# Transfers of ScalarE's results issued by ScalarE itself, in a two-layer attention, delta-rule and Fourier backbone

## The chip, the cores and the metric

The kernel runs on one core of a Trainium2 chip. The metric is the device time of one execution in microseconds; before the change the median of three runs is 2653.78 us. The core's engines work side by side, each through its own queue of instructions in a fixed order: TensorE (PE in the profile) multiplies matrices, VectorE (DVE), ScalarE (ACT) and GpSimd (POOL) do elementwise work, and SyncE (SP) issues transfers between the main memory and the on-chip memory. Semaphores tie the queues together: an instruction that waits for a result of another engine holds up everything behind it on its own.

## The reference: what is computed

512 latent tokens and 256 context tokens, 1024 channels each, pass through two layers. In each layer, one wide projection of the normalised tokens feeds three mixers side by side; their results are gated, merged and added, and a squared-ReLU MLP follows. Cut to what matters here:

```python
h_l = _rmsnorm(x, norm1) * (1 + sc1) + sh1
(na_k, na_v, dn_k, dn_v, dn_a, dn_b, na_q, dn_q, dn_z, fn_u, gate) = _split(h_l @ w_in, ...)
# A: 8x16 neighbourhood attention plus all context keys, one softmax, 8 heads of 64
o_na = _neighbourhood_attention(q * scale, k, v, kc, vc, rpb)
# B: gated delta rule in both directions, 4 heads of 128, in chunks
g = -exp(a_log) * softplus(dn_a + dt_bias);  beta = sigmoid(dn_b)
o_dn = _gated_head_norm(ol_f + ol_b, dn_z, dn_norm)
# C: real part of a 2-D Fourier transform over positions and channels, 4 groups of 128
o_fn = _fourier(fn_u)
# merge
g_na, g_dn, g_fn = split(sigmoid(gate))
y = (g_na * (o_na @ w_na_o) + g_dn * (o_dn @ w_dn_o) + g_fn * (o_fn @ w_fn)) @ w_out
x = x + gt1 * y
x = x + gt2 * (square(relu(rmsnorm(x) @ w_mlp1)) @ w_mlp2)
```

Context tokens go through the same mixers and, in the first layer only, through the merge and the MLP as well; in the second layer they only give keys, values and delta-rule states.

## The kernel before

**Layout and precision.** Activations lie with channels on the partitions and tokens along the free axis: 768 columns, 512 latent and 256 context ones (TT; TL is 512, TC is 256). Every large product is done in three passes with operands split in a rounded main part and a remainder: weights (`wr` as loaded, `whi` and `wlo` as split) and activations (`hh`, `hl`). `wload` (L233 and on) loads a weight block of 128x512 on SP, ScalarE casts it to `whi` (L243), and VectorE or GpSimd makes `wlo` (L246). So each projection on TensorE (`ps_in`, `ps_inc`, L255) waits for a load, a cast on ScalarE and a subtraction.

**Stages.** A layer has a mixing stage (projection and the three mixers, mixed with each other), a merge and an MLP. In mixing, the transform runs first, with the first delta-rule head (`fourier` and `dn_in`). Then four streams run together: the delta rule's steps (`stream_dn`), its preparation (`stream_prep`, `dn_prep`: products of keys, decay factors, triangular solve), the attention (`stream_na`, `na_attn`) and the projections (`stream_in`: queries, keys and values of attention, delta-rule inputs, and the first 16 of the 24 blocks of gates).

**What sets the order.** `by_clock` takes from the four streams in turn, by a clock that the streams advance themselves, and gives delta-rule code a higher priority. A scheduler of the framework then sets the order of each engine's queue: it goes by the code's order and priorities, the waits between instructions and its own cost estimates. Which engine issues a transfer is thus an input to it. Transfers share eight completion semaphores, used in turn by all of them.

**The transfers that the change touches.** All are issued by SP, in one queue with the weight loads:

- L462: the decay sums (`gdr` from `gct`, 48x128), a copy made by ScalarE, once per layer. `dn_prep` reads them back for each head at L542 and L543 (`Df`, `Db`, spread over 128 partitions). GpSimd adds masks (L549 to L551) and ScalarE makes 18 exponentials of 128x128 out of them (L556 to L558).
- L750: the gates (`gpre` from `sgp`), 16 blocks in each layer; a sigmoid in several steps ends on ScalarE (L128). They are read again in the merge.
- L793: the queries. `raw` holds two heads on 64 partitions each. For each half, ScalarE makes the main part `qd` (L790), VectorE the remainder `ql` (L791), and two transfers copy each to the other 64 partitions. The scores (L841, L842) read both.
- L880: the attention's result (`ona` from `o_na`), one store for each of four pairs of heads in a layer; its last part is a copy on ScalarE.
- L961: the transform's result (`ofn`, and `ofnn` for the last 4 rows, from `o_fn`), five tiles for the latent part and, in the first layer, five for the context part; copies on ScalarE.

`gct`, `o_fn` and some others share one small ring of buffers (tag `t2`): a buffer is free again when its store has landed.

In attention, `na_pair` takes two heads at a time: their scores (`ps_s`), a softmax on VectorE and ScalarE (`Pm`, L809 to L820), transposes on TensorE (L825, against `ident`), a copy, and the product with the values (L831).

Of the kernel before, what the change touches and what calls it, by code (L numbers as in the profile page):

```python
# [9 lines left out]
F32 = mybir.dt.float32  # L10
# [7 lines left out]
P = 128  # L18
# [20 lines left out]
FNC, FNW, FAW = (0, TL // 2 + 2), (TL + TC) // 2 + 4, 264  # L39
# [7 lines left out]
def kernel(ctx: ExitStack, tc: tile.TileContext, A: dict, out: bass.AP):  # L47
# [327 lines left out]
    def layer(l):  # L375
        full = l == 0
        segs = ALL if full else LAT
        W = TT if full else TL
# [36 lines left out]
        def gates():  # L415
            ab_f = tp.tile([P, TT], F32, tag="t3", name="ab_f")
            for v, (s0, s1) in enumerate(ALL):
                ps, k0 = (ps_aux("ps_ab"), 0) if l else (begun["ab"][v], KD // 2)
                proj_ab(ps, hh, hl, s0, s1, k0, KD)
                act.copy(ab_f[0:32, s0:s1], ps[0:32, 0:s1 - s0])  # L420
            pab = ps_aux("ps_ab2")
            for j in range(6):
                pe.matmul(pab[:, 16 * j:16 * j + 16], lhsT=ab_f[0:32, j * P:(j + 1) * P], rhs=selab, start=True, stop=True)
            abv = pab[:, 0:96].rearrange("p (j c) -> p j c", c=16)
            for nm in ("z", "g", "beta", "gc", "tot", "egc", "tail", "etot", "t0", "nbe", "btail", "ngc"):
                G[nm] = sm.tile([P, 6, 8], F32, tag="g_" + nm, name="g_" + nm)
            alog = rows[l][:, 0:1, :].to_broadcast([P, 6, 8])
            dtb = rows[l][:, 1:2, :].to_broadcast([P, 6, 8])
            ea = sm.tile([P, 8], F32, tag="g_ea", name="g_ea")
            act.activation(out=ea, in_=rows[l][:, 0, :], func=AF.Exp)  # L430
            dve.tensor_tensor(G["z"], abv[:, :, 0:8], dtb, op=ALU.add)
            dve.tensor_scalar(G["t0"], G["z"], -1.0, None, op0=ALU.mult)
            dve.tensor_tensor(G["btail"], G["z"], G["t0"], op=ALU.max)
            act.activation(out=G["t0"], in_=G["btail"], func=AF.Exp, scale=-1.0)
            act.activation(out=G["t0"], in_=G["t0"], func=AF.Ln, bias=1.0)
            dve.scalar_tensor_tensor(G["t0"], in0=G["z"], scalar=0.0, in1=G["t0"], op0=ALU.max, op1=ALU.add)
            dve.scalar_tensor_tensor(G["g"], in0=G["t0"], scalar=-1.0, in1=ea.unsqueeze(1).to_broadcast([P, 6, 8]),
                                     op0=ALU.mult, op1=ALU.mult)
            sigmoid_into(G["beta"], abv[:, :, 8:16])
            pg = ps_aux("ps_g")  # L440
            gflat = G["g"].rearrange("p j c -> p (j c)")
            for i, m in enumerate((m_ui, m_li, ones)):
                pe.matmul(pg[:, 48 * i:48 * i + 48], lhsT=m, rhs=gflat, start=True, stop=True)
            pgv = pg[:, 0:144].rearrange("p (i j c) -> p i j c", i=3, c=8)
            act.copy(G["gc"][:, :, 0:4], pgv[:, 0, :, 0:4])
            act.copy(G["gc"][:, :, 4:8], pgv[:, 1, :, 4:8])
            act.copy(G["tot"], pgv[:, 2])
            dve.tensor_scalar(G["ngc"], G["gc"], -1.0, None, op0=ALU.mult)
            act.activation(out=G["egc"], in_=G["gc"], func=AF.Exp)
            act.activation(out=G["etot"], in_=G["tot"], func=AF.Exp)  # L450
            dve.tensor_tensor(G["t0"], G["tot"], G["gc"], op=ALU.subtract)
            act.activation(out=G["tail"], in_=G["t0"], func=AF.Exp)
            dve.tensor_tensor(G["btail"], G["beta"], G["tail"], op=ALU.mult)
            dve.scalar_tensor_tensor(G["nbe"][:, :, 0:4], in0=G["egc"][:, :, 0:4], scalar=-1.0, in1=G["beta"][:, :, 0:4],
                                     op0=ALU.mult, op1=ALU.mult)
            dve.tensor_scalar(G["nbe"][:, :, 4:8], G["egc"][:, :, 4:8], -1.0, None, op0=ALU.mult)

            pgt = ps_aux("ps_gt")
            pe.transpose(pgt[0:48, 0:P], G["gc"].rearrange("p j c -> p (j c)"), ident)
            gct = tp.tile([P, 512], F32, tag="t2", name="gct")  # L460
            act.copy(gct[0:48, 0:P], pgt[0:48, 0:P])
            sp.dma_start(out=gdr, in_=gct[0:48, 0:P])  # L462


        odn = drp.tile([NDH, P, TT], F32, tag="odn", bufs=1, name="odn")
# [277 lines left out]
        def pre_gates():  # L743
            for k in range(NPRE):
                ps = inproj(T_GATE + k, segs)
                sg = tp.tile([P, TT], F32, tag="t3", name="sgp")
                gl = U("gl", tag="cy", w=774)
                evac(gl, ps)
                sigmoid_into(sg[:, :W], gl[:, :W])
                sp.dma_start(out=gpre[k, :, :W], in_=sg[:, :W])  # L750
                yield IN_T[l]


# [2 lines left out]
        def na_in(c, st):  # L756

            halves = (slice(0, 64), slice(64, P))
            ps = inproj(T_NAK + c, ALL)
            raw = tp.tile([P, TT], F32, tag="t3", name="kraw")  # L760
            act.copy(raw[:, 0:TL].rearrange("p (t r c) -> p t r c", t=4, c=16),
                     ps[0].rearrange("p (r t c) -> p t r c", r=8, c=16))
            act.copy(raw[:, TL:TT], ps[1][:, 0:TC])
            ks = [U("ks", F32R, tag="n") for _ in range(2)]
            for t, r, r2 in zip(ks, halves, halves[::-1]):
                act.copy(t[r], raw[r])
                dve.tensor_tensor(t[r2], raw[r], t[r].bitcast(F32), op=ALU.subtract)
            yield IN_T[l]
            ps = inproj(T_NAV + c, ALL)
            vN = tp.tile([P, TT], F32, tag="t3", name="vN")  # L770
            act.copy(vN[:, 0:TL].rearrange("p (t r c) -> p t r c", t=4, c=16),
                     ps[0].rearrange("p (r t c) -> p t r c", r=8, c=16))
            act.copy(vN[:, TL:TT], ps[1][:, 0:TC])
            vt = tok_major(vN, OFF, "naV", tag="n")
            yield IN_T[l]
            ps = inproj(T_NAQ + c, segs)
            raw = tp.tile([P, TT], F32, tag="t3", name="qraw")
            pq = ps[0].rearrange("p (r c) -> p r c", c=64)
            act.activation(out=raw[:, P:TL].rearrange("p (t r c) -> p t r c", t=3, c=16),
                           in_=pq[:, :, 8:56].rearrange("p r (t c) -> p t r c", c=16), func=AF.Copy, scale=0.125)  # L780
            act.activation(out=raw[:, 0:P].rearrange("p (r a b) -> p r a b", r=8, b=8),
                           in_=ps[0].rearrange("p (r a b) -> p r a b", r=8, b=8)[:, :, 0:8:7, :], func=AF.Copy,
                           scale=0.125)
            if full:
                act.activation(out=raw[:, TL:TT], in_=ps[1][:, 0:TC], func=AF.Copy, scale=0.125)

            qd = [U("qd", F32R, tag="n") for _ in range(2)]
            ql = [U("ql", F32R, tag="n") for _ in range(2)]
            for t, lo, r, r2 in zip(qd, ql, halves, halves[::-1]):
                act.copy(t[r, :W], raw[r, :W])  # L790
                dve.tensor_tensor(lo[r, :W], raw[r, :W], t[r, :W].bitcast(F32), op=ALU.subtract)  # L791
                for x in (t, lo):
                    sp.dma_start(out=x[r2, :W].bitcast(F32), in_=x[r, :W].bitcast(F32))  # L793
            st.update(ks=ks, vt=vt, qd=qd, ql=ql)
            yield IN_T[l]

# [39 lines left out]
        def na_attn(c, st):  # L836
# [34 lines left out]
            if full:  # L871
                for qi in range(2):
                    def scores(hh):
# [3 lines left out]

                    yield from na_pair(scores, 0, (None, None), [vt[:, 4], vt[:, 5]],
                                       o[:, TL + qi * P:TL + (qi + 1) * P], lambda t: t)
            sp.dma_start(out=ona[c, :, :W], in_=o[:, :W])  # L880

# [4 lines left out]
        def fourier():  # L888
# [35 lines left out]
            for i, (s0, n, tab) in enumerate(sets):  # L924
# [26 lines left out]
                for x, c0, c1 in ((0, 0, P), (0, P, 2 * P), (1, 0, P), (1, P, 2 * P), (0, 256, 260)):  # L951
                    m = c1 - c0
                    ps = ps_aux("ps_fb", "fb")
                    for r, (w, f) in enumerate(ab[x]):
                        for y, (a, b) in enumerate(((0, 0), (0, 1), (1, 0))):
                            pe.matmul(ps[0:m, :nh], lhsT=w[a][:, c0:c1], rhs=f[b][:, :nh], start=(r == 0 and y == 0),
                                      stop=(r == len(ab[x]) - 1 and y == 2))
                    o = tp.tile([P, 512], F32, tag="t2", name="o_fn")
                    act.copy(o[0:m, :nh], ps[0:m, :nh])
                    dst = ofnn if m == 4 else ofn[2 * x + c0 // P]  # L960
                    sp.dma_start(out=dst[:, FNC[i]:FNC[i] + nh], in_=o[0:m, :nh])  # L961
                    yield 2


# [403 lines left out]
```

## Time and profile before

| what | value |
| --- | --- |
| median of three runs | 2653.78 us (2650.65 to 2654.24) |
| the profiled execution | 2646.47 us, of which its span 2644.6 us |
| TensorE busy | 2460.2 us (93%), 14608 matmuls |
| VectorE, ScalarE, GpSimd busy | 1533.8, 1211.9, 650.3 us |
| mean granted TensorE clock | 0.975 of full speed |
| TensorE busy, 100 to 745 us (mixing, layer 0) | 591.58 of 645 us |
| TensorE busy, 1550 to 2117 us (mixing, layer 1) | 504.68 of 567 us |

The busy time of an engine doesn't count what it issues as transfers. Such issues appear as "SPq" in a timeline, that is, as work of SP's sequencer, with the time that the issuing took; when the data have landed is a separate figure. A wait row names the waiting instruction by engine, tile and line, then what came last of all that it waited for, the total in microseconds, how often, and the longest. In a timeline, the bracket at a row's end is the idle time of the engine before it, and what ended it.

### The profile page before, as it was taken

What the parts mean: (1) busy time and instruction counts of PE and PEld (TensorE: products, weight loads), DVE (VectorE), ACT (ScalarE), POOL (GpSimd) and SP (SyncE); (2) the same over time, 40 slices, a digit from 0 to 9 for tenths busy, and PEclk for the clock granted to TensorE, in tenths of its full rate; (3) what the DMA queues carried; (4) which work ended last, traced back from release to release, by engine and by line L of the source; (5) the groups of instructions that cost most, each with busy time, mean ns of one, the idle gap of its engine ahead of it and who ended that gap; (6) DMA issues with size and microseconds to landing.
All of it is one profiled execution on the core that took longest, in us unless ns stands there. A gap on an engine that the chain in (4) does not pass through costs nothing. (4 is left out here: it accounts for less than half of the span.)

```text
span 2644.6 us, 39355 instructions
## 1 busy us (share of the span) xinstructions
PE 2460.2 (93%) x14608; PEld 2039.8 (77%) x14608; DVE 1533.8 (58%) x3035; ACT 1211.9 (46%) x2573; POOL 650.3 (25%) x536
## 2 busy tenths in 40 slices
PE   6988999899998999999999988898889999999998
PEld 3876877777887878888888867676777777788886
DVE  4627676757557967564434473857677457433334
ACT  4545657565654233131313255555566763423333
POOL 3222223231122122111111133322333232222222
PEclk9999999999999999999999999999999999999999
DMA  6233132323154743334333313332222345233332
GB/s 222 67 83 87 60 77 75 86 78 86 55 182 149 225 145 109 126 111 127 119 127 112 124 62 95 86 77 71 75 84 80 99 143 191 80 96 96 96 96 87
DMA packets 188807, 280.90 MB, mean 106 GB/s; under 512 B 57876, under 2 KB 78104, under 8 KB 188488
## 3 DMA queue, kind: packets, MB, share of 16 engines
q1 hardware_dynamic: 188616, 278.40, 34.7%
q8 instruction: 114, 1.87, 0.3%
q14 instruction: 77, 0.63, 0.1%
HBM read 242.86 MB, written 26.03 MB: 102 GB/s over the span
## 5 line engine op out<-in xcount | busy, mean ns | idle before, releaser
L246 POOL TENSOR_TENSOR wlo<-wr,whi 128x512 fp32r<-128x512 f32 x352 | 497.5, 1416 | 1670.5 <-ACT whi L243 1550.0
L243 ACT CAST whi<-wr 128x512 fp32r<-128x512 f32 x544 | 335.5, 619 | 783.6 <-PE ps_m L255 490.8
L255 PE MATMUL ps_in<-hh,whi 128*128 128x512 f32 x960 | 378.2, 405 | 26.9 <-ACT whi L243 21.3
L255 PE MATMUL ps_in<-hh,wlo 128*128 128x512 f32 x960 | 374.3, 400 | 2.6 <-POOL wlo L246 2.5
L255 PE MATMUL ps_in<-hl,whi 128*128 128x512 f32 x960 | 374.7, 401 | 0.0
L255 PE MATMUL ps_m<-mh,whi 128*128 128x512 f32 (+1 forms) x768 | 232.3, 357 | 4.7 <-ACT mh L319 4.7
L255 PE MATMUL ps_m<-ml,whi 128*128 128x512 f32 (+1 forms) x768 | 233.5, 358 | 2.8 <-POOL ml L323 2.3
L255 PE MATMUL ps_m<-ah,whi 128*128 128x512 f32 (+1 forms) x776 | 233.5, 354 | 0.0
L255 PE MATMUL ps_m<-al,whi 128*128 128x512 f32 (+1 forms) x776 | 233.1, 354 | 0.0
L255 PE MATMUL ps_m<-ah,wlo 128*128 128x512 f32 (+1 forms) x776 | 233.0, 354 | 0.0
L255 PE MATMUL ps_m<-mh,wlo 128*128 128x512 f32 (+1 forms) x768 | 232.6, 356 | 0.0
L255 PEld LDWEIGHTS ps_in<-hh,whi 128*128 128x128 f32 x960 | 180.9, 193 | 58.8 <-ACT whi L243 22.3
L246 DVE TENSOR_TENSOR wlo<-wr,whi 128x512 fp32r<-128x512 f32 x192 | 135.7, 707 | 138.7 <-ACT whi L243 138.6
L255 PEld LDWEIGHTS ps_in<-hh,wlo 128*128 128x128 f32 x960 | 180.3, 192 | 37.4 <-POOL wlo L246 5.6
L255 PEld LDWEIGHTS ps_in<-hl,whi 128*128 128x128 f32 x960 | 180.9, 193 | 29.8 <-issue 1.7
L1198 DVE SCALAR_TENSOR_TENSOR x<-ps_m,mod,x 128x512 f32<-128x512 f32 (+1 forms) x97 | 60.8, 654 | 215.4 <-PE ps_m L255 215.4
L202 DVE SCALAR_TENSOR_TENSOR jada<-wada,csb 128x1024 f32<-128x1024 f32 x128 | 179.7, 1404 | 0.8 <-DMA wada<-in_wat_dram 0.4
L255 PEld LDWEIGHTS ps_m<-ml,whi 128*128 128x128 f32 x768 | 127.8, 190 | 27.7 <-POOL ml L323 5.1
L255 PE MATMUL ps_inc<-hh,wlo 128*128 128x256 f32 x512 | 149.2, 291 | 0.0
L255 PE MATMUL ps_inc<-hl,whi 128*128 128x256 f32 x512 | 149.1, 291 | 0.0
L255 PEld LDWEIGHTS ps_m<-mh,whi 128*128 128x128 f32 x768 | 127.8, 190 | 27.6 <-ACT mh L319 6.4
L255 PE MATMUL ps_inc<-hh,whi 128*128 128x256 f32 x512 | 148.7, 290 | 0.1
(338 smaller groups left out, 4962.8 us busy)
## 6 DMA issues: line engine op xcount, KB each, us to landing
wr<-in_w_dram SPq DMA_DIRECT2D x256, 256.0 KB, 2.6
wr<-in_wi_dram SPq DMA_DIRECT2D x224, 256.0 KB, 2.7
wada<-in_wat_dram SPq DMA_DIRECT2D x80, 512.0 KB, 3.9
wr<-in_wb_dram SPq DMA_DIRECT2D x48, 256.0 KB, 3.1
wada<-in_wa_dram SPq DMA_DIRECT2D x32, 256.0 KB, 5.4
wr<-in_wo_dram SPq DMA_DIRECT2D x32, 256.0 KB, 2.8
gpre<-sgp SPq DMA_DIRECT2D x16, 384.0 KB, 2.3
sgg<-gpre SPq DMA_DIRECT2D x16, 384.0 KB, 4.1
```

Of the source, the lines that this page charges most:

```text
L202: pin(dve.scalar_tensor_tensor(junk, in0=ws[n], scalar=1.0, in1=cur["csb"][:, v * D:v * D + D], op0=ALU.mult, op1=ALU.mult, accum_out=MOD[ ...
L243: act.copy(hi, raw)
L246: eng.tensor_tensor(lo, raw, hi.bitcast(F32), op=ALU.subtract)
L255: pe.matmul(ps[:, s0 - off:s1 - off], lhsT=a, rhs=b[k][:, s0:s1], start=(k == 0 and i == 0), stop=(k == kn - 1 and i == 2))
L1198: dve.scalar_tensor_tensor(x2[k][:, s0:s1], in0=ps[:, s0:s1], scalar=mod(l, 5, k, v), in1=x2[k][:, s0:s1], op0=ALU.mult, op1=ALU.add)
```

## The change

Five places take their transfer from SP to ScalarE. At L793, only the main part of the queries moves, which ScalarE makes; the remainder, made by VectorE, stays on SP.

```diff
             act.copy(gct[0:48, 0:P], pgt[0:48, 0:P])
-            sp.dma_start(out=gdr, in_=gct[0:48, 0:P])
+            act.dma_start(out=gdr, in_=gct[0:48, 0:P])
...
                 sigmoid_into(sg[:, :W], gl[:, :W])
-                sp.dma_start(out=gpre[k, :, :W], in_=sg[:, :W])
+                act.dma_start(out=gpre[k, :, :W], in_=sg[:, :W])
...
-                for x in (t, lo):
-                    sp.dma_start(out=x[r2, :W].bitcast(F32), in_=x[r, :W].bitcast(F32))
+
+                for x, q in ((t, act), (lo, sp)):
+                    q.dma_start(out=x[r2, :W].bitcast(F32), in_=x[r, :W].bitcast(F32))
...
-            sp.dma_start(out=ona[c, :, :W], in_=o[:, :W])
+            act.dma_start(out=ona[c, :, :W], in_=o[:, :W])
...
                     dst = ofnn if m == 4 else ofn[2 * x + c0 // P]
-                    sp.dma_start(out=dst[:, FNC[i]:FNC[i] + nh], in_=o[0:m, :nh])
+                    act.dma_start(out=dst[:, FNC[i]:FNC[i] + nh], in_=o[0:m, :nh])
```

Counted over both layers, 2 + 32 + 16 + 8 + 15 = 73 transfers move. The order of the other instructions changes with them, on all engines, within the two mixing stages; the instructions themselves stay the same. A blank line is added, so that from there on line numbers are higher by one in the changed kernel. Three places follow.

SP before the change, at the query copies of the first pair of heads (`qd_1843`, `ql_1845`: first half; `qd_1844`, `ql_1846`: second half):

```order
L240 DMA wr_2720<-in_wi_dram 128x512
L793 DMA qd_1843<-qd_1843 64x768
L793 DMA ql_1845<-ql_1845 64x768
L793 DMA qd_1844<-qd_1844 64x768
L793 DMA ql_1846<-ql_1846 64x768
L240 DMA wr_2726<-in_wi_dram 128x512
```

ScalarE at the same place after the change:

```order
L785 ACTIVATE qraw_1839<-ps_inc_1814 128x256
L790 CAST qd_1843<-qraw_1839 64x768
L794 DMA qd_1843<-qd_1843 64x768
L790 CAST qd_1844<-qraw_1839 64x768
L794 DMA qd_1844<-qd_1844 64x768
L407 COPY gl_2097<-ps_in_2046 128x512
```

The two main parts have gone to ScalarE, each behind its cast; the two remainders now follow each other on SP.

TensorE before the change, layer 1, at the scores of one pair (`ps_s_17053` and `ps_s_17058`, L841 and L842) and their transposes (L825; L493 sums squares for the delta rule's keys):

```order
L841 MATMUL ps_s_17058<-ks_16398,qd_16734 128x256
L842 MATMUL ps_s_17058<-ks_16398,ql_16736 128x256
L825 MATMUL ps_s_17053<-ident_432,Pm_17156 128x128
L493 MATMUL ps_l2_16998<-r_l2_16996,ones_103 128x512
L825 MATMUL ps_s_17053<-ident_432,Pm_17156 128x128 x3
L825 MATMUL ps_s_17058<-ident_432,Pm_17166 128x128
L493 MATMUL ps_l2_17002<-r_l2_16996,ones_103 128x256
```

TensorE after the change, from the last two products of the same scores on:

```order
L842 MATMUL ps_s_17058<-ks_16398,qd_16734 128x256
L843 MATMUL ps_s_17058<-ks_16398,ql_16736 128x256
L255 MATMUL ps_inc_17111<-hh_14406,whi_17076 128x256
L255 MATMUL ps_inc_17111<-hl_14407,whi_17076 128x256
L255 MATMUL ps_inc_17111<-hh_14406,wlo_17077 128x256
L255 MATMUL ps_inc_17111<-hh_14415,whi_17076 128x256
L255 MATMUL ps_inc_17111<-hl_14416,whi_17076 128x256
L255 MATMUL ps_inc_17111<-hh_14415,wlo_17077 128x256
```

and, 10 rows of the same kind later, up to the transposes:

```order
L255 MATMUL ps_inc_17111<-hl_14454,whi_17082 128x256
L255 MATMUL ps_inc_17111<-hh_14453,wlo_17083 128x256
L826 MATMUL ps_s_17053<-ident_432,Pm_17156 128x128 x4
L493 MATMUL ps_l2_16998<-r_l2_16996,ones_103 128x512
L826 MATMUL ps_s_17058<-ident_432,Pm_17166 128x128 x4
L832 MATMUL ps_s_17053<-Pm_17156,naV_16635 64x128
```

A block of a projection (`ps_inc_17111`, the context columns), which stood ahead of the scores, now stands in part between the scores and the transposes, with 18 matmuls.

ScalarE before the change, layer 1, at the end of the transform (`zz` and `sgz` belong to the delta rule's output gate; the block of decay exponentials of `Dl`, `Df`, `Db` comes next):

```order
L959 COPY o_fn_15144<-ps_fb_15137 128x258
L243 CAST whi_15297<-wr_15295 128x512
L407 COPY zz_15197<-ps_in_15172 128x512
L124 ACTIVATE sgz_15198<-zz_15197 128x512
L125 ACTIVATE sgz_15198<-sgz_15198 128x512
L959 COPY o_fn_15157<-ps_fb_15147 4x258
L126 ACTIVATE sgz_15198<-sgz_15198 128x512
```

ScalarE after the change, at the end of that block of exponentials:

```order
L557 ACTIVATE Df_15214<-Df_15214,g_ngc_14534 128x128
L558 ACTIVATE Db_15215<-Db_15215,g_ngc_14534 128x128
L407 COPY gl_15280<-ps_in_15254 128x512
L243 CAST whi_15297<-wr_15295 128x512
L124 ACTIVATE sgp_15279<-gl_15280 128x512
L243 CAST whi_15303<-wr_15301 128x512
L125 ACTIVATE sgp_15279<-sgp_15279 128x512
```

The cast `whi_15297`, which stood ahead of the block, now stands behind it, ahead of the cast `whi_15303`, which stood behind it before, too.

## Rows read from the trace of the kernel before

**Rows 1.** Windows: us from:to, length, busy PE, PEld, DVE, ACT, POOL; clock, DMA share, GB/s.
```profile
100.00:745.00 645.00, 591.58 (x4212) 496.12 (x4210) 400.86 (x1008) 375.68 (x913) 155.82 (x137) 0.97 0.27 77
1550.00:2117.00 567.00, 504.68 (x3377) 402.11 (x3378) 367.89 (x922) 337.54 (x828) 170.26 (x146) 0.96 0.31 84
```

**Rows 2.** Waits of TensorE: waiter, releaser, us in total, times, longest.
```profile
PE ps_s L825 <- DVE Pm L820: 32.6, 20, 6.5
PE ps_in L255 <- ACT whi L243: 21.3, 4, 10.2
...
PE ps_s L841 <- DMA qd<-qd: 3.9, 4, 1.2
```

**Rows 3.** Waits of SP's queue, columns as in rows 2.
```profile
SPq L240 <- POOL wlo L246: 1037.9, 297, 28.3
...
SPq L750 <- ACT sgp L128: 79.1, 25, 7.0
SPq L880 <- ACT o_na L833: 29.8, 5, 11.7
...
SPq L961 <- ACT o_fn L959: 23.1, 12, 6.7
```

**Rows 4.** Tile views of gpre, ofn (two rows), qd: issue in ns, minimum/median/maximum.
```profile
L750 SPq DMA_DIRECT2D gpre<-sgp x32: 320/327/527, 189.0 to 2116.6; - x32
...
L961 SPq DMA_DIRECT2D ofn<-o_fn x12: 319/320/378, 136.4 to 1613.2; - x12
...
DMA to landing us min/median/max: 1.6/2.2/2.4
...
L793 SPq DMA_DIRECT2D qd<-qd x16: 502/529/593, 203.5 to 2018.4; - x16
```

**Rows 5.** Timeline of ScalarE, layer 1: start us, busy us, instruction, idle before.
```profile
1613.04 0.62 ACT L243 CAST whi<-wr 128x512 fp32r<-128x512 f32 x1
...
1624.49 0.61 ACT L128 ACTIVATE sgz<-sgz 128x512 f32<-128x512 f32 x1
...
1625.66 0.69 ACT L558 ACTIVATE Db<-Db,g_ngc 128x128 f32<-128x128 f32 x2 [0.26 <-POOL Db L550]
...
1626.55 0.38 ACT L557 ACTIVATE Df<-Df,g_ngc 128x128 f32<-128x128 f32 x1
1626.84 0.39 ACT L558 ACTIVATE Db<-Db,g_ngc 128x128 f32<-128x128 f32 x1
...
1630.22 0.62 ACT L243 CAST whi<-wr 128x512 fp32r<-128x512 f32 x1
```

**Rows 6.** Timelines of ScalarE (casts) and SP (issues) at the first query copies.
```profile
202.08 1.69 ACT L790 CAST qd<-qraw 64x768 fp32r<-64x768 f32 x2
...
203.53 0.52 SPq L793 DMA_DIRECT2D qd<-qd  x1
...
207.01 0.54 SPq L793 DMA_DIRECT2D qd<-qd  x1
```

**Rows 7.** Timeline of TensorE, layer 1: a pair's last scores and first transpose.
```profile
1804.52 0.28 PE L841 MATMUL ps_s<-ks,qd 128*128 128x256 f32 x1
1804.64 0.28 PE L842 MATMUL ps_s<-ks,ql 128*128 128x256 f32 x1
1811.44 0.45 PE L825 MATMUL ps_s<-ident,Pm 128*128 128x128 f32 x1 [6.52 <-DVE Pm L820]
```

**Rows 8.** Timelines of TensorE around its two longest gaps in mixing.
```profile
166.73 0.80 PE L255 MATMUL ps_in<-hh,whi 128*128 128x512 f32 x1 [10.25 <-ACT whi L243]
...
1618.88 0.48 PE L255 MATMUL ps_in<-hh,whi 128*128 128x512 f32 x1
...
1630.89 0.80 PE L255 MATMUL ps_in<-hh,whi 128*128 128x512 f32 x1 [9.02 <-ACT whi L243]
```

**Rows 9.** Timelines of SP and GpSimd, layer 1: load of decay sums, its first use.
```profile
1611.67 0.38 SPq L542 DMA_DIRECT2D Df<-gdr  x1
...
1619.81 1.84 POOL L549 TENSOR_TENSOR Dl<-Df,n_li 128x768 f32<-128x768 f32 x1 [4.77 <-DMA Df<-gdr]
```

## The prediction

> **What bounds the kernel now.** I read the busy times by stage first, then what TensorE waits for, and only then the queue that the change relieves. The stage table [rows 1] has TensorE busy for 591.58 of the 645 us of the first mixing stage (100 to 745 us) and for 504.68 of the 567 us of the second (1550 to 2117 us). So 53.4 + 62.3 = 115.7 us of it are idle there, and since all edits lie in these stages, no more than that is to be won. TensorE's waits [rows 2] say for what: transposes wait 32.6 us for softmax results, projections 21.3 us for a cast weight, scores 3.9 us for the copied queries. That last one is the only wait for a transfer before TensorE in these stages; neither TensorE nor a cast of ScalarE waits there for a weight load.
>
> SP's queue looks worse than it is. It stood 79.1 + 29.8 + 23.1 = 132 us for results of ScalarE that it had to store [rows 3], and the change takes this away. But it stood 1037.9 us for free weight buffers too: it runs ahead of its consumers and passes from one kind of wait to the other. What covers its blocked time is the weight buffers that are loaded ahead. Were that cover gone, a late load would show as a wait of a cast; there is none, so I cost the freed 132 us at nothing.
>
> **The change part by part.** (a) *Issues on ScalarE.* 73 issues move. One of gate stores (32) takes SP 0.320 to 0.327 us, one of the transform's (12, and 3 small ones) 0.320, one of the query copies (16) 0.529 [rows 4]; attention (8) and decay sums (2) are stores of the first kind. That is 57 x 0.32 + 16 x 0.529 = 26.7 us. The trace of before has no DMA issued by ScalarE, so its own price is open and these rows are the nearest. A store also waits for the result that was just written: ScalarE's instructions overlap by 0.1 us (0.39 us long, 0.29 from start to start, the exponentials of [rows 5]), so a store right behind its result empties that overlap, and I add 0.3 us each for it and for the signal: 22 us. Queued behind are weight casts and softmax steps, and TensorE waits for those. ScalarE is busy 375.68 of 645 and 337.54 of 567 us [rows 1], 59%, so much falls into idle time. TensorE is idle for 115.7 of 1212 us, 9.5%; I let the 48.7 us reach it at that rate: **+4.5**. Ends: 0 if all of it is covered, +24 if every second one hits. ScalarE's issues may also wait for one of SP's transfers, since eight completion semaphores are used in turn by both queues; by the times of before the transfers in question had landed long ago, so 0, and the upper end is a landing, 2.4 us [rows 4].
>
> (b) *Query copies.* Before, the second half's main part stood on SP behind the first half's remainder, which VectorE makes later: SP issued the first main part at 203.53 and the second at 207.01, though both casts were through at 202.08 + 1.69 = 203.8 [rows 6]. Now ScalarE issues each behind its cast, the first some 0.6 us sooner (203.53 against half of the two casts, 202.9). TensorE's four waits for the copies sum to 3.9 us, the longest 1.2 [rows 2]; at 0.6 each I take **-2.5**, ends 0 and -3.9.
>
> (c) *Softmax covers.* The diff doesn't show it, but the order of all engines changes within the mixing stages. Two heads' scores form a pair, 40 pairs in all; TensorE's work between a pair's scores and its transposes is the cover of the softmax on VectorE and ScalarE. In layer 1 one pair has next to none: its last score starts at 1804.64, its transpose at 1811.44, with 6.52 us idle [rows 7]. In the new order 18 matmuls of 256 columns stand in between, 2.2 us at 0.12 us from start to start [rows 7]. Over all 40 pairs I summed what the cover lacks: for a softmax of 4 us 19.0 us before and 11.2 now, for 5 us 35.3 and 27.2, for 3 us 9.4 and 3.9. The wait measured is 32.6 us [rows 2], between the sums for 4 and 5 us: **-8**, ends -5.5 and -8.1 as long as (a) doesn't stretch the softmax itself.
>
> (d) *The large gap of layer 1.* TensorE stands 9.02 us until 1630.89 for a cast weight [rows 8]. ScalarE had cast the weight before that one at 1613.04, ahead of a block of 18 decay exponentials [rows 5], so that TensorE still had 12 matmuls from 1618.88 on [rows 8], 2.7 us at 0.23 each. In the new order that cast stands behind the whole block too. The block can't move up: it waits for GpSimd, which began at 1619.81 when a load of decay sums had landed [rows 9], and whose last product let ScalarE go on at 1625.66; from there to the awaited cast at 1630.22 it took 4.56 us [rows 5]. The new order has two exponentials (0.29 each) and a gate step (0.61) more in that stretch: TensorE goes on 1.2 us later, with 2.7 us of matmuls undone, less 0.36 for two small products that now stand ahead: **+3.5**. Ends +2.5, and +6 if the load lands 2.4 us later.
>
> (e) *The same gap of layer 0*, 10.25 us up to 166.73 [rows 8], has the same cause, and TensorE's order around it stays. Its load of decay sums is written over memory of the transform, so it still waits for the last transform matmul: 0, ends -2 and +1.
>
> Both gaps would shrink if that load landed sooner. In layer 1 it took 8.1 us (issue at 1611.67, GpSimd at 1619.81, [rows 9]), with transform stores just ahead of it and just behind it on the same queue. A transform store lands in 1.6 to 2.4 us [rows 4]; were the load rid of them, up to 2.4 us a gap, -4.8 in all, is the bound. I take 0, since the weight loads stay in that queue. The Trainium skill (DMA: Bandwidth & Descriptors, "Issuing engines are not separate DMA queues") speaks against any such gain: it has the DMAs of all issuing engines run on the same 16 DMA engines and interleave, and only the sequencer's issue time saved. By that page this term is 0, and the faster rival below would end at 2645 instead of 2640; by the bound from the rows it stays -4.8. No run here shows two issuing engines yet.
>
> (f) *Other chains.* Covers counted in the same way, for what needs 1 to 2 us, give +2.2 us for the last products of the delta rule's solve, +2.5 for key transposes, +2.1 for the solve's first products, -3.6 for the delta rule's steps: **+3**, ends -3 and +7. For the two stores of decay sums nobody waits.
>
> The sum: 4.5 - 2.5 - 8 + 3.5 + 0 + 3 = +0.5 us. The profiled execution took 2646.47 us (2644.6 span and 1.9 around it), 7.3 less than the median 2653.78 of the runs shown, which reach from 2650.65 to 2654.24. So 2647.0 for a like execution and **2654 us** as a median. A difference of 0.2%, 5.3 us, is what a measurement here can tell from none.
>
> **The rivals.** *ScalarE becomes what mixing waits for* (slower). Each issue holds up the cast or softmax step behind it, at places where TensorE waits already: the projections' casts and the transposes [rows 2]. For it: ScalarE has a part in both of these waits. Against it: it idles 41% of the time there. It decides from about every third issue that reaches TensorE: then (a) is +16, and (c), with the softmax's own steps stretched, -4. So 16 - 2.5 - 4 + 3.5 + 3 = +16, **2670 us**. *The new order and the free queue pay in full* (faster): issues covered (0), (c) -8, (b) -3.9, (d) +2.5, the loads of decay sums sooner by 4.8, (f) 0: -14, **2640 us**. For it: the softmax is the largest of the waits, and SP issues the delta rule's small loads too, some of them late. Against it: those chains run on VectorE and ScalarE, and TensorE's own wait for a transfer is 3.9 us in all.
>
> **How the numbers follow.** The forecast, within 0.2%: 0.37. Slower, by ScalarE or by covers that fail: 0.32. Faster: 0.31. That the transfers move is plain in the order, so a change that does nothing has no chance here. The range goes from the faster rival's 2640 to the slower one's 2670, with 2 us more at either end for the bounds of (d) and (f): 2638 to 2672.
>
> **What would show it.** (a) ScalarE's queue has 73 issues of 0.3 to 0.5 us; at twice that the slower rival gains. (b) The wait for the query copies falls from 3.9 to about 1.5 us. (c) Transposes wait about 25 us instead of 32.6, and the gap of 6.5 us is near 4. (d) The gap of layer 1 is 12 to 13 us instead of 9.0, that of layer 0 stays near 10. SP's waits for ScalarE are gone, and those for weight buffers have grown by about as much. The forecast is wrong if ScalarE stands at a store until another transfer lands, or if TensorE's idle time in the mixing stages moves from 115.7 us by over 6.

## The result, and the profile after

The changed kernel takes 2669.41 us (median of five runs, 2665.52 to 2672.94) where the kernel before takes 2654.24 (five runs, 2650.65 to 2660.0): a ratio of 1.0055, 95% interval 1.0041 to 1.0069. It is **slower by 15 us**, inside the predicted range, but not the likeliest case. The number is that of the slower rival; the mechanism is another, as the experiments show.

The page of the profiled execution (2670.43 us) begins so; the second line is TensorE's busy time:

```profile
span 2668.0 us, 39335 instructions
PE 2471.6 (93%) x14608; PEld 2049.3 (77%) x14608; DVE 1549.9 (58%) x3035; ACT 1212.2 (45%) x2573; POOL 646.2 (24%) x536
```

Before, the span was 2644.6 us with TensorE busy for 2460.2 of them. So 23.4 us more are 12.0 us of idle time (184.4 to 196.4) and 11.4 us in which the same 14608 matmuls were busy for longer. The windows of the two mixing stages, cut to hold the matmuls of [rows 1], columns as there:

```profile
100.00:760.00 660.00, 599.89 (x4214) 501.49 (x4213) 402.66 (x1008) 377.48 (x915) 152.76 (x137) 0.96 0.27 75
1567.00:2140.00 573.00, 509.04 (x3386) 407.37 (x3385) 383.05 (x923) 337.85 (x831) 168.92 (x148) 0.96 0.29 83
```

Idle in mixing is now 60.1 + 64.0 = 124.1 us, 8.4 more than before, and the first stage's clock went from 0.97 to 0.96. What TensorE waited for, columns as in [rows 2]:

```profile
PE ps_s L826 <- DVE Pm L821: 24.8, 18, 3.6
...
PE ps_in L255 <- ACT whi L243: 14.0, 6, 5.8
...
PE ps_ch L687 <- ACT Uc L685: 9.9, 6, 3.5
PE ps_kk L564 <- DVE PT L573: 9.0, 1, 9.0
...
PE ps_ch L683 <- DVE Z L681: 5.4, 5, 1.6
PE ps_s L843 <- DMA ql<-ql: 5.2, 5, 1.4
...
PE ps_s L826 <- ACT r_l L488: 3.7, 1, 3.7
...
PE ps_ch L683 <- DVE L L653: 3.5, 2, 1.9
...
PE ps_w L643 <- ACT R L640: 2.5, 2, 1.9
PE ps_s L842 <- DMA qd<-qd: 2.1, 2, 1.1
```

The wait for the softmax fell as expected (32.6 to 24.8), but the transposes gained nothing by it: summed over all releasers, like the `r_l` above, their waits are 37.3 us before and 37.3 us now. The delta rule's steps (`ps_ch`), the key products (`ps_kk`) and the remainders of the copied queries (`ql`) have come in. SP's waits for ScalarE [rows 3] are gone, and its wait for weight buffers grew by 73 us, from 1037.9 to:

```profile
SPq L240 <- POOL wlo L246: 1110.8, 303, 30.3
```

An issue costs ScalarE about what it costs SP. Tile views of `gpre` and `qd`, columns as in [rows 4]:

```profile
L750 ACTq DMA_DIRECT2D gpre<-sgp x32: 321/327/358, 190.4 to 2137.7; - x32
...
L794 ACTq DMA_DIRECT2D qd<-qd x16: 468/479/506, 204.3 to 2038.7; - x16
```

A second profile of the unchanged kernel (the run `before_again`, below) has a span of 2651.4 us: 186.2 idle, 2465.2 busy. The profile that the prediction used was 7 us below that. A difference of a few us between two profiles is therefore not read as an effect here; the verdicts rest on the ratios, and profiles say where.

### The profile page after: what moved, and what is told of

Read it like the earlier page. It is cut to its first block, busy times and chain, and to the rows that moved or that the text cites. A ratio compares the mean times of both kernels' runs of the same rounds, so it can differ in the third digit from the quotient of the medians.

```text
span 2668.0 us, 39335 instructions
## 1 busy us (share of the span) xinstructions
PE 2471.6 (93%) x14608; PEld 2049.3 (77%) x14608; DVE 1549.9 (58%) x3035; ACT 1212.2 (45%) x2573; POOL 646.2 (24%) x536
## 5 line engine op out<-in xcount | busy, mean ns | idle before, releaser
L246 POOL TENSOR_TENSOR wlo<-wr,whi 128x512 fp32r<-128x512 f32 x352 | 490.5, 1395 | 1674.4 <-ACT whi L243 1561.3
```

Source lines behind the costliest of these rows:

```text
L246: eng.tensor_tensor(lo, raw, hi.bitcast(F32), op=ALU.subtract)
```

## Experiments

The change does two things at once: it moves 73 issues, and it lets the scheduler order all engines anew. To hold one fixed, these kernels pin the order. After the kernel's body, each instruction gets an order-only edge, without a semaphore, to the one ahead of it in a table of the instructions of each engine:

```diff
+def _pin(tc, nc):
+    ...
+        e.sort(key=lambda i: at[i.name])
+        for a, b in zip(e, e[1:]):
+            tc.add_manual_dep(b, a.name, DependencyInfo(NoSync, DATA), reason="pinned order")
...
         tile_backbone_kernel(tc, aps, o)
+        _pin(tc, nc)
```

With the order of before, a transfer moved to ScalarE stands there where SP had it in time, mostly one to four instructions behind its result; in the traces of the kernels pinned to it, TensorE, VectorE, ScalarE and GpSimd run the same sequence of operations as in the kernel before. All ratios are to the kernel before on the same chip.

**Issue and order apart.** The first kernel has the five edits of the change and the order of before:

```diff
-            sp.dma_start(out=ona[c, :, :W], in_=o[:, :W])
+            act.dma_start(out=ona[c, :, :W], in_=o[:, :W])
...  # and likewise for gdr, gpre, qd, ofn; ORDER = that of the kernel before
```

> The changed kernel with every engine's order pinned to that of the kernel before; the 73 transfers stand on ScalarE where that order sent them, one to four instructions behind the result in most cases. Only the issuing engine differs from before. Theory O (the new order costs the 15 us, the issues themselves are covered): within 4 us of before, 2650 to 2658 us. Theory I (the issues hold up ScalarE and through it TensorE): 2664 to 2672 us, as after the change. If both have a part, between: 2658 to 2664 us.

Measured: 2641.18 us, ratio 0.9953 (0.9938 to 0.9969). The second has no edit of the issues, and the changed kernel's order:

```diff
         tile_backbone_kernel(tc, aps, o)
+        _pin(tc, nc)    # ORDER = that of the changed kernel, SP issues all
```

> The kernel before with every engine's order pinned to that of the changed kernel; the 73 transfers stand on SP's queue where that order sends them. Only the order differs from before. Theory O (the order costs): 2664 to 2672 us, as after the change. Theory I (the issues on ScalarE cost): within 4 us of before, 2650 to 2658 us, or some 4 us below where the new order covers softmax waits better. If both have a part: 2658 to 2664 us. SP's waits for ScalarE's results should be back, at 130 to 140 us.

Measured: 2684.4 us, ratio 1.0113 (1.0093 to 1.0132). Two factors, four cells:

| ratio to before | order of before | order of the change |
| --- | --- | --- |
| SP issues | 1 | 1.0113 |
| ScalarE issues | 0.9953 | 1.0055 |

Issuing on ScalarE gains 12 us in the old order and 15 in the new (1.0113 to 1.0055, each ratio with some 4 to 5 us on either side). The new order costs 30 us with SP's issue and 27 with ScalarE's. The two add up within that, and ScalarE's issue in the old order beats the other three. The issues on ScalarE are not what costs: the slower rival's mechanism has the wrong sign.

One wait follows the issuing engine in either order, TensorE's wait for the delta rule's solve (`ps_w`, for `R`, which ScalarE copies). Before, then the first and the second kernel:

```profile
PE ps_w L643 <- ACT R L640: 14.8, 4, 4.5
...
PE ps_w L643 <- ACT R L640: 10.2, 3, 4.5
...
PE ps_w L643 <- ACT R L640: 9.0, 2, 4.8
```

In the changed kernel it is 2.5. So it falls by 4.6 us with ScalarE's issue in the old order, and by 6.5 in the new.

Windows of the mixing stages of the first kernel:

```profile
100.00:751.50 651.50, 603.29 (x4260) 504.79 (x4259) 405.12 (x1015) 382.09 (x923) 158.14 (x140) 0.97 0.28 80
...
1550.00:2117.00 567.00, 505.32 (x3385) 403.33 (x3384) 370.89 (x923) 338.84 (x831) 165.48 (x148) 0.96 0.30 85
```

of the changed kernel, cut to the same matmuls (its second stage stands above):

```profile
100.00:768.40 668.40, 608.29 (x4261) 508.86 (x4260) 406.18 (x1015) 382.84 (x924) 155.76 (x140) 0.96 0.27 78
```

and of the second kernel:

```profile
100.00:778.40 678.40, 617.54 (x4264) 518.79 (x4264) 404.74 (x1016) 384.22 (x925) 156.15 (x140) 0.94 0.27 77
```

From the first kernel to the changed one, the first stage grows by 16.9 us: idle 48.2 to 60.1, busy by 5.0. The second grows by 6.0: idle 61.7 to 64.0, busy by 3.7. From there to the second kernel, the first stage grows by 10.0, of which idle is 0.8 and busy 9.25, at a mean clock of 0.94 instead of 0.96. So part of what these kernels differ by is not a wait at all: the profile grants TensorE either 2.4 or 1.2 GHz, and a lower mean says that it was at the lower level for longer.

**Which layer's order.** The 73 issues on ScalarE, the new order in one layer and the old in the other:

```diff
+        _pin(tc, nc)    # ORDER: layer 0 of the changed kernel, layer 1 of before
```

> All 73 transfers issued by ScalarE; the new order in layer 0, the order of before in layer 1. Old order in both layers gave 2641 us, the new one in both 2669. The profiles put 17 of the 25 us between those two kernels into layer 0 and 8 into layer 1. If the order's cost lies in each layer by itself: 2641 + 17 = 2658 us, range 2654 to 2663. If it were one place in layer 1 alone (the large gap): 2641 us.

Measured: 2660.8 us, 1.0021 (1.0008 to 1.0034); against the first kernel's 0.9953 that is +18 us.

```diff
+        _pin(tc, nc)    # ORDER: layer 0 of before, layer 1 of the changed kernel
```

> The counterpart: the order of before in layer 0, the new one in layer 1, all 73 transfers issued by ScalarE. By the profiles: 2641 + 8 = 2649 us, range 2645 to 2654. The two parts should add up to the 28 us between the orders; a sum well off that would mean that the layers act on each other, or that the clock makes the difference by chance.

Measured: 2650.62 us, 0.9986 (0.9973 to 0.9998), +9 us. 18 + 9 = 27, what the whole order costs: the layers add up, each with some 5 us on either side. In layer 1 the waits that grow most in sum are those of the delta rule's steps. TensorE's waits in this kernel, and the window of its second mixing stage:

```profile
PE ps_ch L687 <- ACT Uc L685: 8.3, 4, 3.5
...
PE ps_ch L683 <- DVE Z L681: 5.2, 4, 1.6
PE ps_ch L683 <- DVE L L653: 3.7, 2, 2.0
...
1547.00:2121.50 574.50, 506.43 (x3385) 403.97 (x3385) 383.48 (x925) 339.80 (x833) 172.02 (x149) 0.96 0.30 84
```

17.2 us, against 1.8 + 2.0 + 2.6 = 6.4 in the kernel with the old order: 10.8 us more for the delta rule's steps. Not all of it is lost, since other waits shrink (the solve's from 10.2 to 5.3): TensorE's idle time in the stage is 68.1 us against 61.7 for the same 3385 matmuls, 6.4 of the 9 us. In layer 0 the loss is spread over several waits of 1 to 5 us. Which reordered places cause it was tried in neither layer, and stays open.

**Which issues gain.** In the old order, only the queries, only the gates, or only the transform, attention and decay sums on ScalarE:

```diff
+                for x, q in ((t, act), (lo, sp)):
+                    q.dma_start(out=x[r2, :W].bitcast(F32), in_=x[r, :W].bitcast(F32))
```

> Order of before pinned; only the 16 query copies are issued by ScalarE. All 73 together gave 2641 us in this order, 13 below before. Theory Q (the gain is the scores that start sooner): 2643 to 2647 us. Theory G (SP set free from the gates) and theory R (the transform's stores): 2651 to 2656 us here, as before.

Measured: 2654.21 us, 1.0003 (0.9991 to 1.0015). Waits of TensorE there:

```profile
PE ps_s L842 <- DMA ql<-ql: 2.1, 2, 1.5
...
PE ps_s L841 <- DMA qd<-qd: 1.3, 2, 1.1
```

The wait for `qd` falls from 3.9 to 1.3 us, that for `ql`, 0.6 before, takes over: the queries gain nothing, if the pinned order by itself costs nothing. That was not run alone; but the kernel with all but the queries, below, agrees (0.9958 against 0.9953 with them).

```diff
-                sp.dma_start(out=gpre[k, :, :W], in_=sg[:, :W])
+                act.dma_start(out=gpre[k, :, :W], in_=sg[:, :W])
```

> Order of before pinned; only the 32 gate stores are issued by ScalarE. Theory G (SP no longer stands 79 us for gates, so the small loads of the delta rule and the rotations come sooner): 2642 to 2648 us. Theories Q and R: 2651 to 2656 us.

Measured: 2650.49 us, 0.9986 (0.9972 to 1.0).

```diff
+            act.dma_start(out=gdr, in_=gct[0:48, 0:P])
...
+            act.dma_start(out=ona[c, :, :W], in_=o[:, :W])
...
+                    act.dma_start(out=dst[:, FNC[i]:FNC[i] + nh], in_=o[0:m, :nh])
```

> Order of before pinned; the transform's 15 stores, the attention's 8 and the 2 of the decay sums are issued by ScalarE, gates and queries by SP. Theory R (the load of decay sums gets ahead of the transform's stores, so the large gap of layer 0 shrinks from 10.3 to 5 to 7 us): 2646 to 2650 us. Theories Q and G: 2651 to 2656 us.

Measured: 2651.26 us, 0.9988 (0.9975 to 1.0001). Neither theory G nor theory R came out in full: both times lie above their own theory's range, by 2.5 and 1.3 us. And all but the queries:

```diff
                 for x in (t, lo):
                     sp.dma_start(...)    # queries stay on SP; the other 57 on ScalarE
```

> Order of before pinned; gates, transform, attention and decay sums (57 transfers) issued by ScalarE, the query copies by SP. All 73 gave a ratio of 0.9953; queries alone 1.0003, gates alone 0.9986, the rest alone 0.9988. If the parts add up and the queries are worth nothing: 0.9974 or so, 2647 us. If gates and rest act together, since SP stands free only when none of them is left in its queue: as with all 73, 0.995, 2641 us. If the queries matter once SP is free, the ratio stays at 0.997 to 0.998.

Measured: 2643.82 us, 0.9958 (0.9943 to 0.9973). Gates and the rest give 4 and 3 us alone, 11 together; whether they help each other or the intervals (3 to 4 us on either side of each) hide equal sums stays open.

**The same kernel again**, for a second trace:

> The kernel before, unchanged, for a second profile. The first one took 2646.5 us, 8 us less than the median of the other executions. If executions differ in how long TensorE runs at its lower clock, a profile near 2654 us shows more of that time than the first one's 41 and 44 us in the mixing stages, at equal idle time; if they differ in transfers, it shows more idle time.

Measured: one run, 2653.34 us. Idle time is 186.2 us against 184.4, so most of the 6.8 us between the two spans is longer busy time (5.0); by the traces' clock records TensorE is busy at the lower level for 103.6 us against 98.5, which makes about half of it, and the rest stays open. Places of it (timelines of SP, ScalarE, GpSimd and TensorE, in order of time):

```profile
143.55 2.99 SPq L961 DMA_DIRECT2D ofn<-o_fn  x4
146.64 0.37 SPq L542 DMA_DIRECT2D Df<-gdr  x1
...
166.57 0.79 PE L255 MATMUL ps_in<-hh,whi 128*128 128x512 f32 x1 [10.27 <-ACT whi L243]
...
1725.60 0.27 ACT L833 COPY o_na<-ps_s 128x128 f32<-128x128 f32 x1 [0.21 <-PE ps_s L831]
...
1725.89 0.33 SPq L880 DMA_DIRECT2D ona<-o_na  x1
...
1727.24 0.54 SPq L543 DMA_DIRECT2D Db<-gdr  x1
...
1736.71 1.80 POOL L550 TENSOR_TENSOR Db<-Db,n_li 128x768 f32<-128x768 f32 x1 [5.69 <-issue]
...
1738.55 0.69 ACT L558 ACTIVATE Db<-Db,g_ngc 128x128 f32<-128x128 f32 x2 [4.28 <-POOL Db L550]
...
1739.65 0.36 PE L643 MATMUL ps_w<-R,N 64*64 64x64 f32 x1 [3.80 <-ACT R L640]
```

and the same places of the kernel with 73 issues on ScalarE in the old order:

```profile
145.09 0.38 SPq L542 DMA_DIRECT2D Df<-gdr  x1
...
154.08 0.50 PE L255 MATMUL ps_in<-hh,whi 128*128 128x512 f32 x1 [2.06 <-ACT o_fn L959]
165.53 0.80 PE L255 MATMUL ps_in<-hh,whi 128*128 128x512 f32 x1 [4.98 <-ACT whi L243]
...
1718.60 0.54 SPq L543 DMA_DIRECT2D Db<-gdr  x1
...
1730.13 1.82 POOL L550 TENSOR_TENSOR Db<-Db,n_li 128x768 f32<-128x768 f32 x1
...
1733.31 0.68 ACT L558 ACTIVATE Db<-Db,g_ngc 128x128 f32<-128x128 f32 x2
...
1734.95 0.27 PE L643 MATMUL ps_w<-R,N 64*64 64x64 f32 x1
```

In layer 0, SP had stood behind transform stores that waited for ScalarE; the load of decay sums behind them now goes out 1.6 us sooner, and the gap of 10.27 us becomes 2.06 + 4.98. In layer 1 it was an attention store. ScalarE made its result at 1725.60, SP issued the store at 1725.89, and only then the loads of decay sums behind it. With the store on ScalarE's queue the second load goes out at 1718.60 instead of 1727.24, GpSimd adds its mask at 1730.13 instead of 1736.71, ScalarE's exponentials no longer wait 4.28 us for that, the copy of `R` behind them comes sooner, and the solve's wait of 3.80 us is gone. That GpSimd waited for this load is inferred: its row names no releaser, but where the landing of such a load is measured in the kernel before, it comes 6.9 to 8.5 us after the issue. A wait for the solve of 4.72 us in layer 0, at 262 us, stays in both kernels (4.03).

So 3.2 + 3.8 = 7.0 us less of waits have a place. In the kernel with only the transform group on ScalarE both places change too: 2.16 + 5.39 us for the gap, and no wait for the solve there. With only the gates both stay (11.07 and 3.56 us), and so with only the queries (11.13 and 3.47). Not all of it reaches the end: TensorE's idle time as a whole falls by 5.7 us (186.2 to 180.5) of the 8.3 between the two spans, and the kernel with the transform group alone is only 3 us faster, with idle time down by 4.8 us and busy time up by 2.8. What the gates gain has no place that the traces show.

**The large gaps.** The casts of two weights ahead of the block of decay exponentials, in each layer, on top of the first kernel:

```diff
 L126 ACTIVATE sgz<-sgz 128x512
 L961 DMA ofnn<-o_fn 4x258
+L243 CAST whi<-wr 128x512
 L556 ACTIVATE Dl<-Dl,g_gc 128x128
...
 L407 COPY gl<-ps_in 128x512
-L243 CAST whi<-wr 128x512
```

> The pinned order of before with the 73 transfers on ScalarE, and two weight casts with their remainders moved ahead: in each layer, the cast for which TensorE stands in its largest gap comes before the block of decay exponentials instead of behind it. TensorE then has 12 matmuls of 512 and 24 of 256 columns, 5.6 us, to do within each gap of 5 to 10 us. In layer 1 the remainder delays the block by 1.3 us. Expected if the gaps bound TensorE: 5.6 + 4.3 = 10 us less than 2641, with 1 to 3 us more where the shorter gap keeps the clock at its upper level: 2628 to 2633 us. If what follows the gap was bound by the block anyway, 2637 to 2641 us.

Measured: 2636.6 us, 0.9931 (0.9913 to 0.9949), next to the second case. In layer 1, TensorE's timeline:

```profile
1624.01 0.50 PE L255 MATMUL ps_in<-hh,whi 128*128 128x512 f32 x1 [1.13 <-ACT whi L243]
...
1633.70 0.58 PE L255 MATMUL ps_inc<-hh,whi 128*128 128x256 f32 x1 [5.71 <-ACT gl L407]
```

The gap of 9.93 us became 1.13, and 5.71 came back at the next thing behind the block, a copy. So the copy was put ahead as well (`gl`, L407, in layer 1):

> The kernel with the casts ahead of the decay block (ratio 0.9931), with the copy of the gate block in layer 1 ahead of the decay block too: with the casts alone, TensorE's gap there shrank from 9.9 us but the context half then stood 5.7 us for the buffer that this copy frees. Expected if that wait was the next bound: 3 to 5 us less, a ratio of 0.9912 to 0.992, 2631 us. If TensorE then waits for the block's results by as much: 0.993, as without it.

Measured: 2640.45 us, 0.9948 (0.993 to 0.9966), no gain. Now the copy after that is late:

```profile
1637.01 0.80 PE L255 MATMUL ps_in<-hh,whi 128*128 128x512 f32 x1 [6.59 <-ACT kraw L761]
```

and the same with the queries on SP:

> As the kernel with casts and copy ahead, but the 16 query copies issued by SP again. If the queries on ScalarE are worth nothing or cost a little (they hold the second cast back by 0.5 us each): same time or up to 3 us less. If they help once SP is free: 2 to 5 us more.

Measured: 2640.72 us, 0.9947 (0.9928 to 0.9966). All three lie some 14 us or more below the kernel before; none is told apart from the 0.9953 of the first. Work put ahead of the block leaves the next piece late. That fits an end set by the block and its wait for GpSimd; a block that comes sooner was not tried.

## Why the prediction came out as it did

**Where it failed first: SP's freed time was costed at nothing.** The argument was that weight buffers cover SP's waits, since no cast waits for a load. But SP's queue carries the loads of decay sums too, for which GpSimd waits; they stood behind stores waiting for ScalarE. The issue on ScalarE, priced at +4.5 us, is worth -12 to -15 together with the relief of SP. The price of an issue was right (0.33 and 0.48 us); how much of it reaches TensorE no run separates from the relief, which was missing from the sum. The prediction named the load itself, with a bound of -4.8 us, and took 0. With the old order, the gap of layer 0 shrank by 10.25 - 7.04 = 3.2 us, while that of layer 1 did not (9.02 to 9.93), and the solve's wait in layer 1 went, 3.8 us behind an attention store, which no term held. The prediction's list of waits leaves the solve out, though its 14.8 us lie in the mixing stages alone.

The bound itself rested on a misreading. Of the 1.6 to 2.4 us of [rows 4] only the 1.6 is a transform store; the other two are loads of its result in the merge. And the load of decay sums is slow by itself: in layer 1 it took 8.1 us to GpSimd's start with the transform stores in its queue, and 8.0 (1611.36 to 1619.35) with these on ScalarE's. What the change can give is an earlier issue of the load, and where SP waits for ScalarE that is 1.6 to 8.6 us.

**The rule of the Trainium skill weighed there pointed the wrong way.** The Trainium skill (DMA: Bandwidth & Descriptors, "Issuing engines are not separate DMA queues") has only the sequencer's issue time saved, which it calls usually small relative to the DMA itself. Here SP's sequencer also stood at its waits, and the kernel with ScalarE's issue in the old order is 12 us faster. Whether the other half of that rule holds here, that transfers of all issuing engines interleave, can't be told from ScalarE's waits. These are its copies of the transform's last 4 rows, first in that kernel in layer 0, then in the kernel before in layer 1:

```profile
153.77 0.26 ACT L959 COPY o_fn<-ps_fb 4x130 f32<-4x130 f32 x1 [5.78 <-DMA ofn<-o_fn]
...
1620.52 0.36 ACT L959 COPY o_fn<-ps_fb 4x258 f32<-4x258 f32 x1 [5.05 <-DMA ofn<-o_fn]
```

The first copy waits for a transform store while SP's loads of decay sums run; at the same place of the kernel before, where these loads came later, it waited 0.98 us. It is the source of the 2.06 us at 154 us. But the second waits as long with both in SP's queue, the load ahead of the store. That the stores landed late because of those loads is inferred: no landing of theirs is measured.

**Where it failed second: (f), the order's other chains.** It counted -3.6 us for the delta rule's steps. They wait 18.8 us now (9.9 + 5.4 + 3.5), against 4.5 before. It may be that the order spent on the softmax the cover that these steps had. The count of cover took the softmax and the steps at fixed durations and one by one; the steps form a recurrence, in which a late one makes the next late. Both reasons are argued, not shown. What is shown is the size: the order costs 27 to 30 us, where (c) + (d) + (f) gave -1.5.

**What the sum couldn't hold.** It counted idle time alone. Of the 27 us between the first experiment and the changed kernel (24.9 us of span in the profiles), 15.9 are idle, 9.0 are the same matmuls at a lower mean clock. No experiment isolates that part, but the traces' clock records fit it. By them TensorE is busy at the lower level, where a matmul is taken to last twice as long, for 97.7 us in the first kernel, 122.4 in the changed and 153.1 in the second; and in all 14 profiles the busy time less half of that is 2408 to 2414 us, where the busy time itself goes from 2460.2 to 2484.7.

**What was right, and how far.** (c) The wait for the softmax is 24.8 us, as forecast, but the 8 us are not won: the transposes wait as long as before in all. (b) `qd` waits 2.1 us, near the 1.5 forecast, but `ql` takes 5.2: the two together rise from 4.5 to 7.3, where 2.5 less was forecast. ScalarE's timeline shows a part of why:

```profile
203.47 0.84 ACT L790 CAST qd<-qraw 64x768 fp32r<-64x768 f32 x1
204.34 0.51 ACTq L794 DMA_DIRECT2D qd<-qd  x1
204.88 0.83 ACT L790 CAST qd<-qraw 64x768 fp32r<-64x768 f32 x1 [0.58 <-ACT qd L790]
205.75 0.49 ACTq L794 DMA_DIRECT2D qd<-qd  x1
```

The issue stands between the two casts, and the second half's remainder, which needs the second cast, comes that much later. From the first cast's start to the second's end it is 2.24 us, against 1.69 before: 0.55 more for an issue of 0.51, so the 0.3 us that (a) added to each issue does not show here. (d) The gap of layer 1 is now

```profile
1645.09 0.79 PE L564 MATMUL ps_kk<-kT 128*128 128x128 f32 x2 [9.01 <-DVE PT L573]
...
1648.75 0.79 PE L255 MATMUL ps_in<-hh,whi 128*128 128x512 f32 x1 [2.45 <-ACT whi L243]
```

11.5 us in two pieces, against 9.0: +2.5, the low end of what was given. Its first piece has another releaser, but the same block behind it. (e) The gap of layer 0 is 2.56 + 5.78 = 8.3 us, 1.9 less than before and within the ends given.

By its own test the forecast was wrong: idle time in mixing moved by 8.4 us, more than the 6 allowed. The rivals' errors had opposite signs: the issues pay, more than the faster rival held, and the order costs, more than any case held. That the time still lies in the range is luck: an error of some 17 us in the issues (+4.5 against -12) and one of some 29 in the order (-1.5 against +27) cancel in good part.

## What to carry to other kernels

Where a scheduler reorders the program after an edit, pin the order and measure the edit and the order apart: here -12 and +27 us hid in a result of +15. An in-order queue that waits is judged by everything in it, the small loads of other chains first, not by its biggest customer. A forecast from idle time alone leaves out that the same matmuls can be busy for longer under another order: compare busy time of equal matmuls as well. And a wait that falls can come back under another releaser, so sum what an instruction waits for over all of them.

## What the runs showed of the hardware

- An issue on ScalarE takes 0.33 us (median) for a store of a gate tile of 128x768 or 128x512 and 0.48 for a query copy of 64x768 or 64x512; on SP it takes 0.33 and 0.53.
- The load of decay sums, spread over 128 partitions, reached GpSimd 8.1 and 8.0 us after its issue in layer 1, with transform stores in its own queue and in ScalarE's.
- The same 14608 matmuls were busy for 2460.2 to 2484.7 us in these kernels; at the ends the mean granted clock was 0.975 and 0.964: 24 us that no wait shows.
- Two profiles of the same kernel differ by 7 us, 5.0 of it in busy time.
